# Modulation columns of a two-block transformer: raw fp32 weight blocks as the stationary operand instead of split weight rows

## The chip, the cores and the metric

The kernel runs on one core of one Trainium2 chip. The metric is the device time of one execution in microseconds (us). The engines are PE (TensorE, whose weight loads are listed apart as PEld), DVE (VectorE), ACT (ScalarE), POOL (GpSimd) and SP (SyncE, which issues most transfers). The kernel before took 1550.29 us in the median of three runs (1546.9 to 1552.76).

## The reference

Two transformer blocks of two layers each run over 512 tokens (and 256 context tokens) with 1024 features, all in fp32. The first block is modulated. For each of its two layers a condition vector of the tokens and one of the context give 3072 values each:

```
sc, scc = silu(c), silu(c_ctx)
mod   = sc  @ mod_w[i] + mod_b[i]        # [1024] @ [1024, 3072]
mod_c = scc @ mod_w[i] + mod_b[i]
shift, scale, gate = split(mod, 3)
h = rmsnorm(x) * (1 + scale) + shift     # input of the layer's projections
x = x + gate * (mix @ w_out)             # end of the layer
```

Layer AB (i = 0) has two dense attentions and updates tokens and context. Layer CD (i = 1) has a window attention and a short convolution and updates the tokens alone. The second block (an even layer, an odd layer, each with a per-layer embedding) has no modulation, and nothing in it changes.

## The kernel before

**Numbers and layout.** Activations stand feature-major, X[feature, token], each as two parts hi and lo in the reduced fp32r format. A projection multiplies three times per 128 features (hi by hi, lo by hi, hi by lo; lines 238 to 240). Weights arrive as raw fp32 pieces [128, 4, 256] of 512 KB through `weights` (line 210): SP issues the load into one of three buffers `raw`, ACT casts 512 columns to `wh` (line 229), DVE subtracts to get `wl` (line 232), and the raw buffer is free again.

**Modulation.** `mod_w` of a layer is cut into 12 chunks of 256 columns: 0 to 3 shift, 4 to 7 scale, 8 to 11 gate. A chunk is 1 MB, two raw pieces. It is used with the four columns `sc4` (hi and lo of the two conditions) as the stationary operand and 256 weight columns as the moving one: 16 matmuls (hi and lo of 8 feature blocks) into a PSUM row block [4, 256]. DVE copies it to `rows` (line 325 or 340), the bias is row 5, and two small fp32 matmuls with the 5 by 2 selector `sel2` (line 348) sum the parts and turn them into per-feature columns `modT`.

- Layer 0, chunks 0 to 7, run first in `start` (line 641), with buffers of their own: four `mraw`, five `mhi`, five `mlo` (`mod_load`, `mod_first`, lines 303 to 326; matmuls on line 323). The same stage norms and transposes the tokens (line 388), and scales and shifts them feature block by feature block (`fill`, lines 664 to 666). The first projection, `ab_first` (288 columns, 144 matmuls), can use a feature block as soon as it is filled.
- The other 16 chunks are fillers that use the general weight path (`mod_rows`, matmuls on lines 338 and 339): layer 1, chunks 0 to 7, and layer 0, gate chunks 8 to 11, lie between the projections of layer AB; layer 1, gate chunks 8 to 11, lie between items of layer CD's attention (`rest`, paced over 21 units).
- Gate rows take a trip through DRAM: `gate_rows` stores [5, 256] (line 357), `gate_sum` reads [5, 512], sums with `sel2` (line 364, 512 columns moving) and stores [2, 512] (line 366), and `gate_bc` reads one row broadcast to 128 partitions (line 370). `w_out` multiplies its result by the gate (line 906).

**Order.** The program is written in this order, and a scheduler with a model of its own lays out each engine's queue. On the chip each queue runs strictly in that order.

Of the kernel before, what the change touches and what calls it, by code (L numbers as in the profile page):

```python
# [29 lines left out]
class Kern:  # L30
# [55 lines left out]
    def psum(self, **banks):  # L86
        """the four banks beside the two pairs"""
        self.banks = banks
        self.pstack.close()
        self.ps = self.pstack.enter_context(self.pool("ps", space=PSUM))  # L90
# [9 lines left out]
    def setup(self, stack):  # L100
# [8 lines left out]
        self.grow_d, self.gsum_d = ([self.dram.tile([n, 1024], F32, name=f"g{n}row{l}_d") for l in range(2)] for n in (5, 2))  # L109
# [6 lines left out]
        self.sel2 = c.tile([5, 2], F32, name="sel2")  # L116
        nc.scalar.dma_start(out=self.sel2, in_=I["sel"])
        self.sc = c.tile([128, 8, 2], F32, name="sc")
        self.sc4 = c.tile([128, 8, 4], F32R, name="sc4")
        self.ng = c.tile([128, 2, 8], F32, name="ng")  # L120
        nc.scalar.dma_start(out=self.ng, in_=I["norm_g_2"])
        self.modT = [c.tile([128, 16, 2], F32, name=f"modT{l}") for l in range(2)]

    def gain_row(self, pool, name, tag, scale=None):
        """input row [1, n] on every partition"""
# [9 lines left out]
    def rstd(self, ms, n):  # L135
        """ms [128, n] mean squares -> (ms + eps)^-0.5"""
        self.nc.vector.tensor_scalar(out=ms, in0=ms, scalar1=EPS, scalar2=None, op0=ALU.add)  # L137
        self.nc.gpsimd.tensor_tensor(out=ms, in0=ms, in1=self.mhalf[:, 0:n], op=ALU.pow)  # L138
        return ms

    def split(self, src, hi, lo):
        """hi, lo (fp32r) of a fp32 AP (PSUM or SBUF)"""
# [16 lines left out]
    def silu2(self, ps, out):  # L159
        """out = 2*silu(ps)"""  # L160
# [4 lines left out]
    def head_norm(self, ps, H, d):  # L165
        """ps PSUM [128, T, H*d] -> normalised fp32 SBUF [128, T, H, d] (no gain)"""
# [18 lines left out]
    def rope(self, out, xn, C, S, r0, rot):  # L185
        """out = xn*C plus the rotary part on [r0, r0+rot), half-split pairs; C [128, T, d], S [128, T, rot]"""
# [12 lines left out]
    def gain_heads(self, out, xn, g):  # L199
        """out = xn*g over [128, T, H, d]"""  # L200
# [9 lines left out]
    def weights(self, ap):  # L210
        """ap DRAM [128, nk, n] -> [(k0, hi, lo)] pieces in fp32r"""
# [48 lines left out]
    def proj_feat(self, out, X, W, c0, t0, n):  # L260
        """feature-major block: out PSUM [128, n] = W[:, c0:c0+128]^T @ X[:, t0:t0+n]"""
# [20 lines left out]
    def feat(self, X, W, t=512):  # L282
        """feature blocks of a chunk over t tokens: yields (b, PSUM [128, n], t0, n)"""
# [9 lines left out]
    def load_silu_c(self):  # L293
# [7 lines left out]
        self.split(self.sc, self.sc4[:, :, 0:2], self.sc4[:, :, 2:4])  # L301

    def mod_load(self, layer, ch, pool):
        """the loads of a mod chunk, ahead of mod_first"""
        rows = self.tl(pool, [5, 256], "rows", 4)
        self.nc.scalar.dma_start(out=rows[4:5, :], in_=self.I["mod_b"][layer:layer + 1, 256 * ch:256 * ch + 256])
        raws = []
        for k in (0, 4):
            raws.append(self.tl(pool, [128, 4, 256], "mraw", 4))
            self.nc.sync.dma_start(out=raws[-1], in_=self.I["mod_w"][layer, ch][:, k:k + 4, :])  # L310
        return rows, raws

    def mod_first(self, ld, pool):
        """rows [5, 256] (x, ctx hi parts, lo parts, bias) of a loaded mod chunk"""
        nc = self.nc
        rows, raws = ld
        p = self.B()
        for kk in range(8):
            if kk % 2 == 0:
                hi, lo = (self.tl(pool, [128, 2, 256], x, 5, F32R) for x in ("mhi", "mlo"))  # L320
                self.split(raws[kk // 4][:, kk % 4:kk % 4 + 2, :], hi, lo)
            for j, w in enumerate((hi, lo)):
                nc.tensor.matmul(out=p[0:4, 0:256], lhsT=self.sc4[:, kk, :], rhs=w[:, kk % 2, :], start=kk + j == 0,
                                 stop=kk == 7 and j == 1)
        nc.vector.tensor_copy(out=rows[0:4, :], in_=p[0:4, 0:256])
        return rows, self.sel2

    def mod_rows(self, layer, ch):
        """rows [5, 256] (x, ctx hi parts, lo parts, bias) of mod chunk ch"""
        nc = self.nc  # L330
        W = self.weights(self.I["mod_w"][layer, ch])
        rows = self.T4([5, 256])
        nc.scalar.dma_start(out=rows[4:5, :], in_=self.I["mod_b"][layer:layer + 1, 256 * ch:256 * ch + 256])
        p = self.B()
        for k0, hi, lo in W:
            for k in range(hi.shape[1]):
                kk = k0 + k
                nc.tensor.matmul(out=p[0:4, 0:256], lhsT=self.sc4[:, kk, :], rhs=hi[:, k, :], start=kk == 0, stop=False)
                nc.tensor.matmul(out=p[0:4, 0:256], lhsT=self.sc4[:, kk, :], rhs=lo[:, k, :], start=False, stop=kk == 7)
        nc.vector.tensor_copy(out=rows[0:4, :], in_=p[0:4, 0:256])  # L340
        return rows, self.sel2

    def mod_cols(self, layer, ch, rs):
        """per-feature columns modT[layer][:, 2*ch + b, (x, ctx)]; the scales with one added"""
        rows, sel = rs
        p = self.B()
        for b in range(2):
            self.nc.tensor.matmul(out=p[:, 2 * b:2 * b + 2], lhsT=rows[:, 128 * b:128 * b + 128], rhs=sel)
        self.nc.vector.tensor_scalar(out=self.modT[layer][:, 2 * ch:2 * ch + 2, :].rearrange("p b e -> p (b e)"),
                                     in0=p[:, 0:4], scalar1=1.0, scalar2=1.0 if ch >= 4 else 0.0,  # L350
                                     op0=ALU.mult, op1=ALU.add)

    def gate_rows(self, layer, chs):
        """rows [5, 256] of the gate's chunks, spilled"""
        for h in chs:
            rows, _ = self.mod_rows(layer, 8 + h)
            self.nc.sync.dma_start(out=self.grow_d[layer][:, 256 * h:256 * h + 256], in_=rows)

    def gate_sum(self, layer, bank="F"):
        """rows [2, 1024] (x, ctx) of the gate from its spilled parts, spilled"""  # L360
        for h in (0, 512):
            rows, r, p = self.T4([5, 512]), self.T4([2, 512]), self.B(bank)
            self.nc.sync.dma_start(out=rows, in_=self.grow_d[layer][:, h:h + 512])
            self.nc.tensor.matmul(out=p[0:2, :], lhsT=self.sel2, rhs=rows)
            self.nc.scalar.copy(out=r, in_=p[0:2, :])
            self.nc.sync.dma_start(out=self.gsum_d[layer][:, h:h + 512], in_=r)

    def gate_bc(self, layer, out, which=0):
        """out[which] [128, 1024]: the gate (of x or ctx) broadcast over the partitions"""
        self.nc.sync.dma_start(out=out[which], in_=self.gsum_d[layer][which:which + 1, :].to_broadcast([128, 1024]))  # L370

# [10 lines left out]
    def transposes(self, xn, g):  # L382
        """PSUM [128, 2, 256]: feature blocks 2g, 2g+1 of two token tiles"""
# [8 lines left out]
    def feat_pair(self, xs, X, t0, scale=None, shift=None, norm=True):  # L392
        """xs: two [128, 1024] token tiles -> X[:, :, t0:t0+256] = (rms(x)*scale + shift)^T, split;
        scale(k), shift(k): per-feature columns"""
# [25 lines left out]
    def tr_pieces(self, src, T, d, fn, kind="R"):  # L420
        """transposes of token-major tiles src(t) [128, d] in PSUM pieces of up to 4 tiles: fn(piece, t0, n)"""
# [1340 lines left out]
def layout(inp):  # L1762
# [5 lines left out]
    d = {}  # L1768
# [73 lines left out]
```

## Time and profile before

| | |
|---|---|
| runs, median (lowest to highest) | 1550.29 us (1546.9 to 1552.76) |
| span of the profiled execution | 1546.3 us |
| its own time beside the span | not listed apart; the runs' median is 4.0 us above the span |
| PE busy, PEld busy | 1486.4 us (96%), 1373.0 us (89%) |
| DVE, ACT, POOL busy | 1036.5 us (67%), 846.5 us (55%), 546.9 us (35%) |
| chain that ended last | PE 79%, DVE 8%, DMA 5%, ACT 3% |
| moved by DMA | 168.20 MB, mean 109 GB/s |

Busy is the union of an engine's instructions. Matmuls overlap, so the time that one costs is the distance from its start to the start of the next, not its own length. A weight load (PEld) overlaps the matmul before it. PEclk is the clock granted to TensorE as a share of 2.4 GHz; it has two levels, 1.2 and 2.4 GHz. The first 19 us have no record of it, and the views print 1.00 there.

### The profile page before, as it was taken

The page shows a single profiled execution, that of the slowest core. Times are in us where ns is not written, and L with a number is a line of the kernel's source. Part 1 is how long each engine was busy: PE and PEld are TensorE (multiplying, and loading weights), DVE is VectorE, ACT ScalarE, POOL GpSimd, SP SyncE. Part 2 cuts the span into 40 slices and gives each one's busy share as a digit, 9 for nine tenths or more (in the row PEclk, how much of TensorE's full clock was granted, in tenths as well). Part 3 has the DMA queues.
Part 4 walks back from the last instruction along what each step waited for, and adds up shares of the span by engine and source line. Part 5 has one row for each costly group of instructions (what it writes and reads, how often), then busy time and mean ns, then how long its engine had stood idle before and what let it go on. Part 6 is the DMA issues. An engine that isn't in the chain of part 4 may idle for free.

```text
span 1546.3 us, 28606 instructions
## 1 busy us (share of the span) xinstructions
PE 1486.4 (96%) x10760; PEld 1373.0 (89%) x10760; DVE 1036.5 (67%) x2121; ACT 846.5 (55%) x1759; POOL 546.9 (35%) x652
## 2 busy tenths in 40 slices
PE   6899999989999999999999999999999999999998
PEld 3799788877998999888889889998899999998998
DVE  6777887889886477777755458986544465565444
ACT  6545555689996154565643446557433544455322
POOL 1533533567674033232421434444201334443000
PEclk8999999999999999999999999999999999999999
DMA  8344564121221332322234222124334321223423
GB/s 304 121 128 120 183 203 162 45 103 33 63 70 31 146 121 71 101 96 86 93 115 145 80 96 82 66 86 137 116 103 143 119 94 57 82 69 132 148 90 110
DMA packets 60685, 168.20 MB, mean 109 GB/s; under 512 B 9890, under 2 KB 18530, under 8 KB 60546
## 3 DMA queue, kind: packets, MB, share of 16 engines
q1 hardware_dynamic: 54768, 163.52, 31.8%
q10 hardware_dynamic: 5778, 2.84, 0.7%
q8 instruction: 85, 1.39, 0.4%
q14 instruction: 54, 0.44, 0.1%
HBM read 144.06 MB, written 22.28 MB: 108 GB/s over the span
## 4 chain that ended last, share of the span: by engine, by line
PE 79%; DVE 8%; DMA 5%; ACT 3%; issue 2%; POOL 2%; SPq 0%; ACTq 0%; DVEq 0%; POOLq 0%
PE A L240 17%; PE A L238 17%; PE A L239 17%; PE B L524 3%; PE F L238 3%; PE F L239 3%; PE F L240 3%; PE F L595 2%; PE B L238 2%; PE B L239 2%; PE B L240 2%; DVE wl L232 1%; PE B L996 1%; PE B L388 1%; PE B L1168 1%
## 5 line engine op out<-in xcount | busy, mean ns | idle before, releaser
L229 ACT CAST wh<-raw 128x512 fp32r<-128x512 f32 (+1 forms) x388 | 232.4, 616 | 237.8 <-PE A L240 166.9
L232 DVE TENSOR_TENSOR wl<-raw,wh 128x512 fp32r<-128x512 f32 (+1 forms) x320 | 233.4, 744 | 93.9 <-ACT wh L229 90.7
L481 POOL TENSOR_SCALAR P<-P,s 128x768 f32<-128x768 f32 (+3 forms) x192 | 152.8, 801 | 176.4 <-DVE s L1264 33.4
L144 DVE TENSOR_TENSOR PTl<-B,PTh 128x512 fp32r<-128x512 f32 (+2 forms) x208 | 127.9, 633 | 47.7 <-ACT PTh L143 35.0
L232 POOL TENSOR_TENSOR wl<-raw,wh 128x512 fp32r<-128x512 f32 x68 | 90.9, 1338 | 158.3 <-ACT wh L229 132.0
L138 POOL TENSOR_TENSOR s8f<-s8f,mhalf 128x4 f32<-128x4 f32 (+2 forms) x53 | 61.5, 1161 | 227.3 <-DVE s8f L137 119.7
L238 PE MATMUL A<-wh,mh 128*128 128x256 f32 x480 | 136.5, 285 | 2.9 <-ACT mh L143 2.9
L143 ACT CAST PTh<-B 128x512 fp32r<-128x512 f32 (+2 forms) x208 | 108.2, 545 | 53.8 <-PE B L524 27.1
L239 PE MATMUL A<-wl,mh 128*128 128x256 f32 x480 | 136.0, 284 | 0.0
L240 PE MATMUL A<-wh,g 128*128 128x256 f32 x408 | 115.7, 285 | 1.2 <-DVE g L144 1.2
L240 PE MATMUL A<-wh,h2l 128*128 128x256 f32 x384 | 108.7, 286 | 2.5 <-DVE h2l L408 2.5
L238 PE MATMUL A<-wh,h4h 128*128 128x256 f32 x384 | 109.5, 286 | 1.0 <-ACT h4h L407 0.8
L240 PE MATMUL A<-wh,h4l 128*128 128x256 f32 x384 | 108.7, 285 | 0.5 <-DVE h4l L408 0.5
L238 PE MATMUL A<-wh,h2h 128*128 128x256 f32 x384 | 108.9, 284 | 0.3 <-ACT h2h L407 0.3
L239 PE MATMUL A<-wl,h4h 128*128 128x256 f32 x384 | 108.7, 284 | 0.0
L239 PE MATMUL A<-wl,h2h 128*128 128x256 f32 x384 | 108.6, 283 | 0.0
L238 PEld LDWEIGHTS A<-wh,mh 128*128 128x128 f32 x480 | 91.9, 192 | 4.3 <-ACT mh L143 3.3
L239 PEld LDWEIGHTS A<-wl,mh 128*128 128x128 f32 x480 | 92.0, 192 | 0.1
L524 PE MATMUL B<-ident,P 128*128 128x128 f32 x592 | 86.2, 274 | 4.5 <-DVE PTl L144 2.4
L240 PEld LDWEIGHTS A<-wh,g 128*128 128x128 f32 x408 | 78.0, 192 | 1.7 <-DVE g L144 1.7
L490 ACT ACTIVATE P<-A,s 128x768 f32<-128x768 f32 (+1 forms) x96 | 73.2, 766 | 7.4 <-DVE s L488 4.7
L524 PEld LDWEIGHTS B<-ident,P 128*128 128x128 f32 x592 | 67.5, 141 | 9.2 <-POOL P L481 2.5
(515 smaller groups left out, 4914.8 us busy)
## 6 DMA issues: line engine op xcount, KB each, us to landing
raw<-mod_w SPq DMA_DIRECT2D x32, 512.0 KB
raw<-even_w SPq DMA_DIRECT2D x32, 512.0 KB
raw<-odd_w SPq DMA_DIRECT2D x32, 512.0 KB
raw<-cd_w SPq DMA_DIRECT2D x26, 512.0 KB
mraw<-mod_w SPq DMA_DIRECT2D x16, 512.0 KB
raw<-w_ple_gate SPq DMA_DIRECT2D x16, 512.0 KB
raw<-ab_wg SPq DMA_DIRECT2D x8, 512.0 KB
raw<-ab_wo SPq DMA_DIRECT2D x8, 512.0 KB
```

The costliest lines, as they stand in the source:

```text
L138: self.nc.gpsimd.tensor_tensor(out=ms, in0=ms, in1=self.mhalf[:, 0:n], op=ALU.pow)
L143: self.nc.scalar.copy(out=hi, in_=src)
L144: self.nc.vector.tensor_tensor(out=lo, in0=src, in1=f32(hi), op=ALU.subtract)
L229: nc.scalar.copy(out=hi, in_=r)
L232: eng.tensor_tensor(out=lo, in0=r, in1=f32(hi), op=ALU.subtract)
L238: mm(out=out, lhsT=xh, rhs=wh, start=start, stop=False)
L239: mm(out=out, lhsT=xh, rhs=wl, start=False, stop=False)
L240: mm(out=out, lhsT=xl, rhs=wh, start=False, stop=stop)
L481: self.nc.gpsimd.tensor_scalar(out=P, in0=P, scalar1=s, scalar2=0.0, op0=ALU.mult, op1=ALU.add)
L490: nc.scalar.activation(out=P[:, u, :], in_=S[:, u, :], func=AF.Exp, bias=m[:, u:u + 1], scale=1.0, accum_out=s[:, u:u + 1])
L524: nc.tensor.transpose(out=pt[:, j, u, :], in_=b, identity=self.ident)
L595: nc.tensor.matmul(out=O, lhsT=vst(e, j), rhs=pts[j // 2][w][:, j % 2], start=w + j == 0, stop=w == 1 and j == nk - 1)
```

## The change

The modulation no longer makes parts of its weights. A raw fp32 block of 128 features by 128 columns is now the stationary operand, and the two fp32 condition columns `sc` stream: 8 fp32 matmuls for each of the chunk's two column blocks, 16 in a chunk, straight into columns [128, 2]. Gone are the ACT casts and DVE subtractions of all 24 chunks, the rows, `sel2` and the DRAM trip. The bias is a table `mb` with one added to the scales beforehand, and one DVE addition writes `modT`, which now holds the gate's columns too. Chunks 0 to 7 of layer 0 have ten `mraw` buffers instead of four. The other 16 chunks take the three shared `raw` buffers, which PE reads directly. `gate_bc` spreads gate columns by four transposes for each half of the 1024 columns. (All comments were removed as well, so line numbers differ: 238 to 240 become 237 to 239, 388 becomes 353, 426 becomes 391.)

```diff
 # setup
-        self.grow_d, self.gsum_d = (...)
-        self.sel2 = c.tile([5, 2], F32, name="sel2")
-        self.sc4 = c.tile([128, 8, 4], F32R, name="sc4")
+        self.mb = c.tile([128, 2, 24], F32, name="mb")
+        nc.scalar.dma_start(out=self.mb, in_=I["mod_bt"])
+        nc.vector.tensor_scalar(out=self.mb[:, :, 8:16], in0=self.mb[:, :, 8:16], scalar1=1.0, scalar2=None, op0=ALU.add)
-        self.modT = [c.tile([128, 16, 2], F32, name=f"modT{l}") for l in range(2)]
+        self.modT = [c.tile([128, 24, 2], F32, name=f"modT{l}") for l in range(2)]
...
+    def mod_load(self, layer, ch, pool=None):
+        raws = []
         for k in (0, 4):
-            raws.append(self.tl(pool, [128, 4, 256], "mraw", 4))
+            raws.append(self.tl(self.rawp, [128, 4, 256], "raw") if pool is None else self.tl(pool, [128, 4, 256], "mraw", 10))
             self.nc.sync.dma_start(out=raws[-1], in_=self.I["mod_w"][layer, ch][:, k:k + 4, :])
...
-    def mod_first(self, ld, pool):
-    def mod_rows(self, layer, ch):
+    def mod_cols(self, layer, ch, raws):
         p = self.B()
         for b in range(2):
-            self.nc.tensor.matmul(out=p[:, 2 * b:2 * b + 2], lhsT=rows[:, 128 * b:128 * b + 128], rhs=sel)
+            for k in range(8):
+                self.nc.tensor.matmul(out=p[:, 2 * b:2 * b + 2], lhsT=raws[k // 4][:, k % 4, 128 * b:128 * b + 128],
+                                      rhs=self.sc[:, k, :], start=k == 0, stop=k == 7)
+        self.nc.vector.tensor_tensor(out=self.modT[layer][:, 2 * ch:2 * ch + 2, :],
+                                     in0=p[:, 0:4].rearrange("p (b e) -> p b e", b=2),
+                                     in1=self.mb[:, layer, 2 * ch:2 * ch + 2].unsqueeze(2).to_broadcast([128, 2, 2]), op=ALU.add)
-    def gate_rows(self, layer, chs):
-    def gate_sum(self, layer, bank="F"):
     def gate_bc(self, layer, out, which=0):
-        self.nc.sync.dma_start(out=out[which], in_=self.gsum_d[layer][which:which + 1, :].to_broadcast([128, 1024]))
+        for h in range(2):
+            t = self.T4([128, 512])
+            self.nc.vector.tensor_copy(out=t.rearrange("p (b f) -> p b f", b=4),
+                                       in_=self.modT[layer][:, 16 + 4 * h:20 + 4 * h, which].unsqueeze(2).to_broadcast([128, 4, 128]))
+            p = self.B("T")
+            for b in range(4):
+                c = slice(128 * b, 128 * b + 128)
+                self.nc.tensor.transpose(out=p[:, c], in_=t[:, c], identity=self.ident)
+            self.nc.scalar.copy(out=out[which][:, 512 * h:512 * h + 512], in_=p)
...
 # start
-            self.mod_cols(0, order[j], self.mod_first(lds[j], mp))
+            self.mod_cols(0, order[j], lds[j])
 # run: the calls between the projections of layer AB
-            self.gate_rows(0, range(4))
-            self.gate_sum(0)
+            self.mods(0, 8, 9, 10, 11)
 # run: layer CD
-                        self.gate_rows(1, (h,))
+                        self.mods(1, 8 + h)
-                self.gate_sum(1)
-            self.pace(items, ru, 21)
+            self.pace(items, ru, 20)
```

Where the queues change is seen at three places. On PE at the end of the first stage, `mhi` and `mlo` are the parts of a chunk, `hTh` is the filled input, and A is the first projection's PSUM. Before, the projections began between the matmuls of the third of the eight chunks:

```order
L323 MATMUL B_372<-mlo_382,sc_82 4x256
L323 MATMUL B_372<-mhi_389,sc_82 4x256
L238 MATMUL A_718<-wh_682,hTh_122 128x288
L323 MATMUL B_372<-mlo_390,sc_82 4x256
L323 MATMUL B_372<-mhi_389,sc_82 4x256
L323 MATMUL B_372<-mlo_390,sc_82 4x256
L323 MATMUL B_372<-mhi_397,sc_82 4x256
```

In the changed program the last of the eight chunks (B_444) ends, and then the first projection starts:

```order
L314 MATMUL B_444<-sc,mraw_414 128x2 x3
L314 MATMUL B_444<-sc,mraw_412 128x2 x4
L314 MATMUL B_444<-sc,mraw_414 128x2 x4
L237 MATMUL A_536<-wh_500,hTh_118 128x288
L238 MATMUL A_536<-wl_501,hTh_118 128x288
L353 MATMUL F_274<-ident,t_40_152 128x128
```

All projections now stand behind all eight chunks, and 40 of the 48 transposes of tokens stand among the chunks.

On PE at the gate chunks of layer 0 (F is the one PSUM bank of the fillers, B_2847 a projection of the latent attention), before:

```order
L338 MATMUL F_2980<-wh_2974,sc_82 4x256
L339 MATMUL F_2980<-wl_2975,sc_82 4x256
L238 MATMUL B_2847<-whf_2789,lTh_949 128x256
L239 MATMUL B_2847<-wlf_2790,lTh_949 128x256
L240 MATMUL B_2847<-whf_2789,lTl_950 128x256
```

The changed program has the last two gate chunks nearly side by side, with only transposes beside them:

```order
L391 MATMUL B_2987<-ident,q_1545 128x128 x4
L314 MATMUL F_2566<-sc,raw_2562 128x2 x4
L314 MATMUL F_2566<-sc,raw_2564 128x2 x4
L314 MATMUL F_2566<-sc,raw_2562 128x2 x4
L314 MATMUL F_2566<-sc,raw_2564 128x2 x4
L391 MATMUL B_2996<-ident,q_1545 128x128 x2
L314 MATMUL F_2588<-sc,raw_2584 128x2 x4
L314 MATMUL F_2588<-sc,raw_2586 128x2 x4
```

Each chunk now reads its two raw buffers twice, so both stay taken until its second half.

On SP's queue at the same place, before, stores of gate rows (`g5row_d`) stood between the loads:

```order
L357 DMA g5row_d<-t_592_2896 5x256
L222 DMA raw_3009<-mod_w 128x1024
L357 DMA g5row_d<-t_604_2937 5x256
L222 DMA raw_3054<-ab_wg 128x1024
L222 DMA raw_3064<-ab_wg 128x1024
L363 DMA t_630_3040<-g5row_d 5x512
```

Now five loads stand in a row, each waiting for one of three buffers that PE itself has to give back:

```order
L816 DMA qkv_d_96<-mk_2427 128x1152
L306 DMA raw_2564<-mod_w 128x1024
L306 DMA raw_2584<-mod_w 128x1024
L306 DMA raw_2586<-mod_w 128x1024
L221 DMA raw_2606<-ab_wg 128x1024
L221 DMA raw_2616<-ab_wg 128x1024
```

The row stores and sums are gone, and the load of the next gate projection's weights waits behind the chunks.

## Rows read from the trace of the kernel before

**Rows 1.** The page, part 1: busy us, share of the span, instructions of each engine.
```profile
PE 1486.4 (96%) x10760; PEld 1373.0 (89%) x10760; DVE 1036.5 (67%) x2121; ACT 846.5 (55%) x1759; POOL 546.9 (35%) x652
```
**Rows 2.** Busy time of each engine in stretches, with PEclk; columns in the first row.
```profile
core 0: us, PE busy (x) PEld busy (x) DVE busy (x) ACT busy (x) POOL busy (x), PEclk, DMA share, GB/s
20.00:80.00 60.00, 51.30 (x338) 42.40 (x339) 46.58 (x87) 37.90 (x74) 25.61 (x23) 0.86 0.56 188
80.00:240.00 160.00, 155.33 (x1109) 138.78 (x1109) 127.69 (x308) 85.70 (x171) 60.74 (x62) 1.00 0.51 163
600.00:790.00 190.00, 188.78 (x1105) 160.87 (x1105) 139.32 (x304) 111.22 (x244) 61.66 (x83) 1.00 0.26 86
```
**Rows 3.** PE's waits, 0 to 80: line waited for, total us, times, longest.
```profile
PE B L323 <- ACT mhi L143: 7.5, 2, 7.2
PE B L348 <- DVE rows L325: 3.6, 5, 2.1
PE B L323 <- DVE mlo L144: 3.1, 3, 2.1
```
**Rows 4.** PE's waits, 80 to 240 (first of five), then 600 to 790 (both).
```profile
PE A L240 <- DVE wl L232: 1.5, 1, 1.5
...
PE F L238 <- ACT cc L1017: 0.8, 1, 0.8
PE F L238 <- DVE t2f L340: 0.3, 1, 0.3
```
**Rows 5.** Timeline near the start: start us, length, engine, line, operation.
```profile
6.55 0.62 ACT L143 CAST mhi<-mraw 128x512 fp32r<-128x512 f32 x1 [2.31 <-DMA mraw<-mod_w]
8.34 0.41 PE L323 MATMUL B<-mlo,sc 128*4 128x256 f32 x1
8.55 0.41 PE L323 MATMUL B<-mhi,sc 128*4 128x256 f32 x1
11.81 0.92 PEld L348 LDWEIGHTS B<-sel,rows 5*128 5x128 f32 x4 [1.00 <-DVE rows L325]
```
**Rows 6.** Timeline at 103 to 105 us and at 235.7 us.
```profile
103.27 0.52 PEld L348 LDWEIGHTS F<-sel,t 5*128 5x128 f32 x4
104.03 0.28 PE L240 MATMUL A<-wh,hTl 128*128 128x256 f32 x1
104.15 0.28 PE L238 MATMUL A<-wh,hTh 128*128 128x256 f32 x1
...
235.72 1.01 PE L364 MATMUL F<-t,sel 5*2 5x512 f32 x2
236.66 0.73 PE L240 MATMUL A<-hTh,wl 128*128 128x512 f32 x2
```
**Rows 7.** Groups by form, PE and PEld: count, busy us, mean ns.
```profile
L348 PE MATMUL B<-sel,rows 5*128 5x2 f32 x32 | 5.5, 273 | 3.6 <-DVE rows L325 3.6
L239 PEld LDWEIGHTS A<-qk,qk 96*128 96x128 f32 x80 | 15.2, 190 | 1.3
L348 PEld LDWEIGHTS F<-sel,t 5*128 5x128 f32 x32 | 4.1, 185 | 1.7 <-DVE wl L232 0.4 <-DVE s8f L844 0.4 <-DVE g L163 0.2
```
**Rows 8.** Timeline: PE in the first projection, one early row and its last.
```profile
70.51 0.29 PE L238 MATMUL A<-wh,hTh 128*128 128x288 f32 x1
...
73.58 0.29 PE L240 MATMUL B<-wh,hTl 128*128 128x288 f32 x1
```
**Rows 9.** Stretches around one fall of the clock, columns as in rows 2.
```profile
74.00:77.00 3.00, 1.38 (x10) 0.71 (x9) 1.80 (x3) 1.93 (x4) 1.93 (x3) 1.00 0.63 210
77.00:81.00 4.00, 4.00 (x23) 4.00 (x22) 3.01 (x10) 3.25 (x9) 1.67 (x4) 0.57 0.80 299
81.00:100.00 19.00, 17.79 (x151) 17.26 (x151) 16.41 (x48) 9.19 (x20) 8.58 (x12) 1.00 0.34 96
```
**Rows 10.** By tile: the gate's use and its broadcast; ns min/median/max, first to last us.
```profile
L906 DVE TENSOR_TENSOR t<-A,gate x20: 680/683/692, 507.8 to 843.8; 128x512 f32<-128x512 f32 x20
L370 SPq DMA_DIRECT2D gate<-g2row_d x3: 325/326/430, 498.7 to 795.8; - x3
```

More of the change, by code (lines that the diff above doesn't have):

```diff
@@ L108, in setup @@
         self.dram = ent(self.pool("dram", space=DRAM))
-        self.grow_d, self.gsum_d = ([self.dram.tile([n, 1024], F32, name=f"g{n}row{l}_d") for l in range(2)] for n in (5, 2))
         self.rot_d = [self.dram.tile([128, 4, 2, n], F32, name=f"rot{n}_d") for n in (16, 32)]
@@ L115, in setup @@
         nc.vector.memset(self.mhalf, -0.5)
-        self.sel2 = c.tile([5, 2], F32, name="sel2")
-        nc.scalar.dma_start(out=self.sel2, in_=I["sel"])
         self.sc = c.tile([128, 8, 2], F32, name="sc")
-        self.sc4 = c.tile([128, 8, 4], F32R, name="sc4")
+        self.mb = c.tile([128, 2, 24], F32, name="mb")
+        nc.scalar.dma_start(out=self.mb, in_=I["mod_bt"])
+        nc.vector.tensor_scalar(out=self.mb[:, :, 8:16], in0=self.mb[:, :, 8:16], scalar1=1.0, scalar2=None, op0=ALU.add)
         self.ng = c.tile([128, 2, 8], F32, name="ng")
         nc.scalar.dma_start(out=self.ng, in_=I["norm_g_2"])
-        self.modT = [c.tile([128, 16, 2], F32, name=f"modT{l}") for l in range(2)]
+        self.modT = [c.tile([128, 24, 2], F32, name=f"modT{l}") for l in range(2)]
     def gain_row(self, pool, name, tag, scale=None):
@@ L300, in load_silu_c @@
         nc.vector.tensor_tensor(out=self.sc, in0=th, in1=ct, op=ALU.mult)
[L301 to L306, printed above, removed]
+    def mod_load(self, layer, ch, pool=None):
         raws = []
         for k in (0, 4):
-            raws.append(self.tl(pool, [128, 4, 256], "mraw", 4))
+            raws.append(self.tl(self.rawp, [128, 4, 256], "raw") if pool is None else self.tl(pool, [128, 4, 256], "mraw", 10))
@@ L310, in mod_load @@
             self.nc.sync.dma_start(out=raws[-1], in_=self.I["mod_w"][layer, ch][:, k:k + 4, :])
-        return rows, raws
-    def mod_first(self, ld, pool):
[L315 to L326, printed above, removed]
@@ L328, in mod_rows @@
-    def mod_rows(self, layer, ch):
[L330 to L341, printed above, removed]
@@ L343, in mod_cols @@
-    def mod_cols(self, layer, ch, rs):
-        rows, sel = rs
+        return raws
+    def mod_cols(self, layer, ch, raws):
         p = self.B()
         for b in range(2):
-            self.nc.tensor.matmul(out=p[:, 2 * b:2 * b + 2], lhsT=rows[:, 128 * b:128 * b + 128], rhs=sel)
-        self.nc.vector.tensor_scalar(out=self.modT[layer][:, 2 * ch:2 * ch + 2, :].rearrange("p b e -> p (b e)"),
-                                     in0=p[:, 0:4], scalar1=1.0, scalar2=1.0 if ch >= 4 else 0.0,
-                                     op0=ALU.mult, op1=ALU.add)
@@ L353, in gate_rows @@
-    def gate_rows(self, layer, chs):
-        for h in chs:
-            rows, _ = self.mod_rows(layer, 8 + h)
-            self.nc.sync.dma_start(out=self.grow_d[layer][:, 256 * h:256 * h + 256], in_=rows)
-    def gate_sum(self, layer, bank="F"):
[L361 to L366, printed above, removed]
@@ new lines, in mods @@
+    def mods(self, layer, *chs):
+        for ch in chs:
+            self.mod_cols(layer, ch, self.mod_load(layer, ch))
+    def gate_bc(self, layer, out, which=0):
+        for h in range(2):
[7 more added lines that the diff above has]
+            self.nc.scalar.copy(out=out[which][:, 512 * h:512 * h + 512], in_=p)
@@ L740, in ab_q @@
         return q
-    def mods(self, *chs):
-        for ch in chs:
-            self.mod_cols(1, ch, self.mod_rows(1, ch))
     def ab_lat(self, X, L, latg, between):
@@ L1479, in proj @@
                 self.banks["F"] = ("F", 1)
-            self.ab_lat(X, L, latg, lambda: self.mods(0, 1))
-            self.mods(2, 3)
+            self.ab_lat(X, L, latg, lambda: self.mods(1, 0, 1))
+            self.mods(1, 2, 3)
             proj(0)
@@ L1485, in run @@
             proj(1)
-            self.mods(4, 5)
+            self.mods(1, 4, 5)
             self.ab_gates(X, 2, keep(4))
             proj(2)
-            self.mods(6, 7)
+            self.mods(1, 6, 7)
             self.ab_gates(X, 3, keep(6))
             proj(3)
-            self.gate_rows(0, range(4))
-            self.gate_sum(0)
+            self.mods(0, 8, 9, 10, 11)
             self.ab_gates(X, 0, spill(0))
@@ L1639, in rest @@
                         yield
-                self.gate_sum(1)
-                yield
                 for b, p, t0, n in self.feat(Xx, self.weights(I["cd_w"][9])):
@@ L1770, in layout @@
     d["ct"] = A(np.stack([g["c"][0], g["c_ctx"]], -1).reshape(8, 128, 2).transpose(1, 0, 2))
-    d["mod_w"], d["mod_b"] = np.stack([chunks(w) for w in g["mod_w"]]), A(g["mod_b"])
+    d["mod_w"] = np.stack([chunks(w) for w in g["mod_w"]])
+    d["mod_bt"] = A(g["mod_b"].reshape(2, 24, 128).transpose(2, 0, 1))
     ab = g["ab_w_in"][0]
@@ L1809, in layout @@
     d["rope_ab"] = A(rope.reshape(4, 128, -1).transpose(1, 0, 2))
-    d["sel"] = np.array([[1, 0], [0, 1], [1, 0], [0, 1], [1, 1]], f)
     neg = f(-1e30)
```

## The prediction

> **What bounds the kernel now.** I read the page's busy times first. The reader is to see PE at 96% and every other engine far below [rows 1]. Then the stretches: from 80 to 240 us and from 600 to 790 us, where 16 of the 24 chunks are worked, PE is busy for 155.33 of 160 and 188.78 of 190 us at the full clock [rows 2]. Before 80 us it is not the only bound: PE has 51.30 of 60 us and a mean clock of 0.86. The waits say who feeds PE. Up to 80 us the splits and row copies of the modulation make it wait 7.5, 3.6 and 3.1 us, 14.2 us in all [rows 3]; from 80 to 240 us there are five waits with 4.5 us together, the longest 1.5, and from 600 to 790 us two with 1.1 us [rows 4]. So behind 80 us what the change frees on ACT and DVE is worth little, and what it adds on PE counts almost one for one.
>
> **PE's price of a chunk.** Before, a chunk is 16 matmuls of 256 columns. At the full clock one follows another after 0.12 us (104.03 to 104.15) [rows 6]: 1.9 us. The new matmul has not run here with 128 rows, but its form has: the selector matmul is plain fp32, 128 stationary columns, two moving columns. It shows 32 loads and 32 matmuls on each bank where the program has 16 (eight chunks, two each) [rows 7]: one fp32 matmul becomes two loads and two matmuls. Four loads take 0.52 us, the last being 0.185 long, so the spacing is (0.52 - 0.185) / 3 = 0.112 us [rows 6, 7]. That the selector has 5 rows and the weights 128 should not matter: a load of 96 rows and 128 columns has 190 ns, one of 5 rows and 128 columns 185 [rows 7]. So a chunk becomes 32 pairs, 32 x 0.112 = 3.6 us at the full clock. At the lower clock four loads take 0.92 us, and matmuls of 256 columns lie 0.21 us apart instead of 0.12 [rows 5, 6]: I take 0.22 for a pair and 7.0 us for a chunk.
>
> **The 16 chunks behind 80 us, at the full clock.** Added: 16 x 3.6 = 57.3 us, and 24 gate transposes, priced as one 128-column load each, 2.7 us. Removed: 256 matmuls x 0.12 = 30.7 us; the selectors of eight chunks, 32 x 0.112 = 3.6 us; the gate sums, eight instructions at (236.66 - 235.72) / 2 = 0.47, 3.8 us [rows 6]. Sum: +22 us. The new matmuls stand as solid blocks of 16, so no other engine's work covers them. Bounds: +15 if a matmul follows a load some 10% sooner than the selector's, +30 if the turn to other work adds 0.5 us a chunk.
>
> By the Trainium skill's page Perfetto Trace Analysis, section "Identifying the Most-Contended Engine", it is the busy share of weight loads that tells PE's room, and not that of matmuls. That share is 89% here [rows 1]; if the 11% left took up these loads, the +22 would be 0. The added loads come in blocks, and the waits in these stretches sum to 5.6 us, so I don't go by it.
>
> **The clock behind 80 us.** From 74 to 77 us PE had 1.38 us of work in 3, and from 77 to 81 the mean granted clock is 0.57; in 81 to 100, with PE working all along, it is 1.00 again [rows 9]. That fall cost 4.00 x 0.43 = 1.7 us. A new chunk keeps the loader busy but streams two columns per load. No row shows loads alone. I expect the clock to treat such a block as idleness. Eight blocks stand alone or first in their group: 1.7 us each. The other eight follow another within some 30 instructions, as the last gate chunks do, and meet the lower clock: half of their pairs at double price (1.8) and 1.7 more, 3.5 us. Together 42, taken as +40 us. Bounds: 0, and 16 x (3.6 + 1.7) = 85 if every block runs wholly at 1.2 GHz.
>
> **The first stage.** PE can begin at 6.6 us, when the first cast began for its landed load [rows 5]. Now it holds eight chunks and 40 transposes ahead of the first projection. Nothing in them streams, so I expect 1.2 GHz throughout: 8 x 7.0 + 40 x 0.22 = 64.8 us, to 71.4 us. Then 144 matmuls of 288 columns, 0.133 us each ((73.58 - 70.51) / 23) [rows 8], 19.2 us, eight transposes 0.9, and 2 us until the clock is up: 93.5 us, where the trace has 73.9. That is +20 us, although the 14.2 us of waits are gone: before, most of the projection ran between the chunks. Bounds: -12 (2.4 GHz nearly from the start: 6.6 + 28.7 + 4.5 + 2 + 20.1 = 62) and +25.
>
> **Smaller terms.** Relief of ACT and DVE: -4, bounds 0 and the 5.6 us of waits. The raw buffers: a chunk reads its first piece until three quarters of it and the second to the end, and SP's queue now has five loads behind one another, each waiting for PE; the next gate projection's weights stand behind them, and `qkv_d` stores too. A load from issue to use took some 4 us at the start (the first cast began at 6.55) [rows 5], a chunk takes 3.6 to 7, so most of it hides: +4, bounds 0 and +20. The DRAM trip: 0. The broadcasts were issued from 498.7 us, the gate is first used at 507.8 [rows 10]; now DVE's copy and ACT's copy for each half lie beside projections. The longer use of PSUM bank F: 0, since one use replaces two.
>
> **Sum.** 22 + 40 + 20 - 4 + 4 = +82 us on a span of 1546.3, so 1628; the runs' median lies 4 us above that span, and the forecast is 1632 us.
>
> **Rivals.**
> (1) The clock stays up, because loads count as work. For it: PE never waits in these blocks. Against it: nothing here shows it either way but the fall after thin work. The start gains 12, the relief 4, the rest costs 22, and the buffers, with nothing to hide them, 7: +13, 1563 us. The Trainium skill's page TensorE: Matmul & The Clock Gate, Part 1, says the gate sets the clock by how busy PE has been; read so that loads are busy, it speaks for this rival. No run here shows a stretch of loads alone.
> (2) The clock is low in the first stage only, and the blocks later are too short to bring it down: 20 + 22 - 4 + 5 = +43, 1593 us. For it: each block is 3.6 us with dense work on both sides. Against it: gate chunks side by side.
> (3) Faster. A matmul with 128 rows needs one load and not two, so a chunk is 16 x 0.112 = 1.8 us. Behind 80 us: 28.7 + 2.7 - 38.1 = -7; the first stage at 1.2 GHz ends 28 us sooner, -8; relief -4, buffers +4: -15, 1535 us; with the clock up throughout 1525. It decides where a pair costs under 0.07 us. Against it: two loads for one selector matmul.
>
> **How the numbers follow.** Forecast 60%, its own range 1600 to 1660; rival 1 18%, with a spread of 15 us around 1563; rival 2 12%; rival 3 7%; 3% for worse than the forecast's range. The range to 80% reaches down into rival 1: 1560 to 1665. A measurement of this kernel can tell about 0.5%, 7.8 us. Faster by more: rival 3 and nothing else, 0.07. Within: the lower edge of rival 1, 0.06. Slower: 0.87.
>
> **What would show it.** The new matmul line should have 768 matmuls and 768 loads, 0.11 us apart at the full clock and 0.22 in the first stage. PEclk should stand near half up to some 75 us, and below 1 in the slices around the chunks. The last 288-column matmul should come near 93 us. ACT's and DVE's share should fall while PE's waits hardly change. The forecast is wrong if PEclk is full while the chunks run, if a matmul shows one load, or if PE waits for raw loads more than 20 us.

## The result and the profile after

The changed kernel takes 1619.34 us (median of 4 runs, 1613.01 to 1622.0) beside 1548.6 us before (4 runs, 1546.44 to 1552.76): a ratio of 1.044, 95% interval 1.0418 to 1.0462, so 70.7 us slower. The forecast was 1632 us. The profiled execution has a span of 1611.2 us, 64.9 more than before's 1546.3; parts below are in terms of these two spans. The profiled execution is the fastest of the four, with a mean granted clock of 0.972; the other three have 0.965 to 0.970 and are 5.6 to 9.0 us longer, so a typical run pays more for the clock than the parts below show.

The page of the changed kernel, busy us with share of the span and count, and the row of the clock in 40 slices of 40.3 us:

```profile
PE 1560.9 (97%) x11096; PEld 1472.1 (91%) x11096; DVE 971.1 (60%) x2015; ACT 796.8 (49%) x1664; POOL 529.2 (33%) x652
...
PEclk9998897999999999998899999999999999999999
```

Beside [rows 1], PE has 74.5 us more, DVE 65 us and ACT 50 us less. The digit of the clock is below 9 in slices 4, 5, 7, 19 and 20 (121 to 201, 242 to 282 and 725 to 806 us), which is where most of the 16 later chunks stand.

The changed kernel by source line, for the new matmul's line: engine, operation, tiles, count, then duration in ns (min/median/max), first and last start, and below what stood idle ahead of it and until what (us, times; this list counts a wait of the loads and one of the matmuls behind them as two):

```profile
L314 PEld LDWEIGHTS F<-sc,raw x512: 186/192/338, 109.9 to 802.2; 128*128 128x128 f32 x171
L314 PE MATMUL F<-sc,raw x512: 165/251/373, 110.0 to 802.3; 128*128 128x2 f32 x171
L314 PEld LDWEIGHTS B<-sc,mraw x256: 288/333/370, 7.7 to 69.4; 128*128 128x128 f32 x128
L314 PE MATMUL B<-sc,mraw x256: 213/352/353, 7.7 to 69.5; 128*128 128x2 f32 x128
...
  DMA mraw<-mod_w: 7.7, 1
  issue: 7.7, 1
  DMA raw<-mod_w: 4.4, 2
  DVE modT L316: 2.1, 2
```

There are 512 + 256 = 768 loads and 768 matmuls for 384 in the program, so each fp32 matmul became two of both, as read from the selector [rows 7]. The eight chunks of the first stage (B) have loads of 333 ns, the later ones (F) 192.

PE on the changed kernel's timeline (start, us, line, tiles, count), in the first stage, at the end of the first projection, and in the first two later chunks:

```profile
42.50 5.12 PE L314 MATMUL B<-sc,mraw 128*128 128x2 f32 x24
47.48 0.88 PE L353 MATMUL F<-ident,t 128*128 128x128 f32 x3
...
91.50 0.30 PE L239 MATMUL B<-wh,hTl 128*128 128x288 f32 x1
...
110.81 3.19 PE L314 MATMUL F<-sc,raw 128*128 128x2 f32 x28
114.35 1.21 PE L726 MATMUL B<-ident,t 128*128 128x128 f32 x4 [0.36 <-DVE t L721]
115.35 2.99 PE L314 MATMUL F<-sc,raw 128*128 128x2 f32 x14
```

At 110.8 us 28 matmuls take 3.19 us, (3.19 - 0.25) / 27 = 0.109 us each: the full clock. At 42.5 us 24 take 5.12, (5.12 - 0.35) / 23 = 0.207: the lower clock. At 115.4 us, one chunk later, 14 take 2.99, (2.99 - 0.35) / 13 = 0.203. These means are a little low, because the first step behind other work is short (0.03 us at the full clock, 0.07 at the lower). Step by step, nearly all matmuls of the new line follow one another after 0.111 or 0.112 us at the full clock and after 0.213 at the lower one. So the block at 110.8 us ran at 2.4 GHz and the next one at 1.2. The last matmul of 288 columns starts at 91.5 us; before it was at 73.6 [rows 8].

Busy time of each engine in the changed kernel in the stretches of [rows 2], and one more around the two chunks above:

```profile
core 0: us, PE busy (x) PEld busy (x) DVE busy (x) ACT busy (x) POOL busy (x), PEclk, DMA share, GB/s
20.00:80.00 60.00, 60.00 (x303) 59.98 (x304) 17.78 (x39) 17.45 (x32) 11.26 (x12) 1.00 0.37 146
80.00:240.00 160.00, 158.04 (x1118) 153.33 (x1117) 95.34 (x246) 58.14 (x120) 61.66 (x71) 0.90 0.39 132
600.00:790.00 190.00, 182.10 (x1154) 164.12 (x1153) 126.68 (x269) 91.20 (x195) 51.92 (x69) 0.96 0.25 82
109.00:125.00 16.00, 15.64 (x97) 15.39 (x96) 4.74 (x11) 4.34 (x8) 0.69 (x1) 0.68 0.40 132
```

From 80 to 240 us the clock is 0.90 and from 600 to 790 0.96, where both were 1.00 [rows 2]. The 1.00 of the first stretch is not a reading: this execution has no record of the clock until 73.6 us, and views print 1.00 where there is none. The step of 0.213 us is what tells the clock there: it is the step that the same pairs have where the record shows 1.2 GHz. The loader is busy for 59.98 of 60 us in it.

**Where the 64.9 us are.** I cut both traces at matmuls that exist in both, and counted each matmul in between at its full-clock step (work; 0.1186 us for 256 columns, 0.233 for 512, 0.112 for a new pair). Where the clock record or the spacing shows 1.2 GHz I added what its step is longer there (clock; 0.213 instead of 0.1186, 0.427 instead of 0.233, 0.213 instead of 0.112), and took the rest as waiting. In us, after minus before:

| stretch, ending at | length | work | clock | waiting |
|---|---|---|---|---|
| last 288-column matmul | +17.9 | +9.9 | +22.8 | -14.8 |
| the rest of the AB projections (280 to 328 us) | +30.1 | +16.0 | +22.3 | -8.2 |
| dense attention and `w_out` of AB, gate transposes | +3.0 | +1.5 | +1.5 | 0.0 |
| layer CD, to its last projection (793 to 862 us) | +18.2 | +5.8 | +10.1 | +2.3 |
| everything behind it | -4.4 | +0.9 | -2.0 | -3.2 |

### The profile page after: what moved, and what is told of

The parts are those of the page before. It is cut to its first block, busy times and chain, and to the rows that moved or that the text cites. A ratio compares the mean times of both kernels' runs of the same rounds, so it can differ in the third digit from the quotient of the medians.

```text
span 1611.2 us, 28851 instructions
## 1 busy us (share of the span) xinstructions
PE 1560.9 (97%) x11096; PEld 1472.1 (91%) x11096; DVE 971.1 (60%) x2015; ACT 796.8 (49%) x1664; POOL 529.2 (33%) x652
## 4 chain that ended last, share of the span: by engine, by line
PE 76%; DVE 7%; DMA 4%; ACT 4%; issue 2%; POOL 2%; SPq 0%; ACTq 0%; DVEq 0%; POOLq 0%
PE A L237 16%; PE A L239 16%; PE A L238 16%; PE B L489 3%; PE F L314 3%; PE F L237 3%; PE F L238 3%; PE F L239 3%; PE F L560 2%; PE B L237 1%; PE B L238 1%; PE B L239 1%; DMA raw<-cd_w 1%; DVE wl L231 1%; PE B L956 1%
## 5 line engine op out<-in xcount | busy, mean ns | idle before, releaser
L228 ACT CAST wh<-raw 128x512 fp32r<-128x512 f32 (+1 forms) x324 | 195.0, 614 | 246.7 <-PE A L239 152.2
L231 DVE TENSOR_TENSOR wl<-raw,wh 128x512 fp32r<-128x512 f32 (+1 forms) x256 | 187.0, 745 | 125.8 <-ACT wh L228 116.4
L446 POOL TENSOR_SCALAR P<-P,s 128x768 f32<-128x768 f32 (+3 forms) x192 | 147.3, 773 | 268.2 <-DVE s L938 72.9
```

The source lines that it names most:

```text
L228: nc.scalar.copy(out=hi, in_=r)
L231: eng.tensor_tensor(out=lo, in0=r, in1=f32(hi), op=ALU.subtract)
L446: self.nc.gpsimd.tensor_scalar(out=P, in0=P, scalar1=s, scalar2=0.0, op0=ALU.mult, op1=ALU.add)
```

## The experiments

The theory: a chunk costs PE two loads for each matmul, and blocks of such loads that stream two columns bring the clock to 1.2 GHz, in them and on either side. The rivals: PE waits for raw buffers and the DMA queue; the first stage is late because projections stand behind all eight chunks, whatever the clock; and, once the first runs were in, that something moves the whole program which is neither.

### One suspected cost taken away: more columns under the same loads

After, and each new matmul streams the two columns 64 times over, 128 columns in all; the loads and the buffers are as in after. The scheduler laid PE's queue out anew for it: some 600 of the 11,096 matmuls stand at another place, and 2 of the 144 matmuls of the first projection now stand ahead of the last chunk's end.

```diff
-                self.nc.tensor.matmul(out=p[:, 2 * b:2 * b + 2], lhsT=raws[k // 4][:, k % 4, 128 * b:128 * b + 128],
-                                      rhs=self.sc[:, k, :], start=k == 0, stop=k == 7)
+                self.nc.tensor.matmul(out=p[:, 256 * b:256 * b + 128].rearrange("p (r e) -> p r e", e=2), lhsT=...,
+                                      rhs=self.sc[:, k, :].unsqueeze(1).to_broadcast([128, 64, 2]), start=k == 0, stop=k == 7)
```

> The changed kernel, but each modulation matmul streams 128 columns instead of two: the two condition columns read 64 times over (a stride of zero), of which only the first two results are used. Loads, order of the code and buffers stay. Theory (the clock falls because these blocks stream almost nothing): PEclk is near 1 in the first stage and in all chunks, a pair costs 0.11 to 0.12 us everywhere, the last 288-column matmul comes at 61 to 66 us instead of 91.5, the half-clock time of about 39 us behind it goes, together -60 to -68 us: 1551 to 1560 us. Rival A (double loads and their place in the order are the whole cost, the clock follows from something else): within 8 us of 1619. Rival B (the loss behind 90 us is PE waiting for raw buffers that it holds itself): the first stage gains 28, the rest stays: about 1590.

Measured: 1565.33 us (1559.6 to 1566.82), ratio to before 1.0083 (1.0056 to 1.011), 54 us less than after; mean clock 0.993 where after has 0.972 (without a record for its first 73.6 us, which count as full there). This kernel's stretches, its new line in the first stage, a chunk, and its last 288-column matmul:

```profile
20.00:80.00 60.00, 58.37 (x484) 57.59 (x483) 35.98 (x84) 25.61 (x51) 26.67 (x34) 1.00 0.51 183
80.00:240.00 160.00, 151.45 (x1129) 143.40 (x1127) 93.06 (x231) 59.23 (x122) 52.97 (x54) 0.99 0.47 152
```
```profile
L314 PEld LDWEIGHTS B<-sc,mraw x256: 188/191/333, 7.8 to 47.4; 128*128 128x128 f32 x128
L314 PE MATMUL B<-sc,mraw x256: 272/273/551, 7.8 to 47.5; 128*128 128x128 f32 x128
```
```profile
66.44 0.29 PE L239 MATMUL B<-wh,hTl 128*128 128x288 f32 x1
...
86.05 2.62 PE L314 MATMUL F<-sc,raw 128*128 128x128 f32 x22
```

The reader sees the same 256 loads end at 47.4 us and not at 69.4, with 191 ns each and not 333, and 0.99 in the second stretch. A pair costs (2.62 - 0.27) / 21 = 0.112 us, as it did at the full clock with two columns: the spacing shows no price for 126 more columns under each load. So 54 of the 71 us are the clock, and the clock came back with more columns streamed, with not one load less. The other order of PE's queue is not kept apart by this run; the two kernels with only the first stage changed, further below, do that. It missed the range of its expectation by 5 us upward, and the last 288-column matmul by 0.4 us. PE's waits for raw loads rose to 5.0 us in four waits (there was one of 2.2). That faster blocks ask for the next buffer sooner would explain it; no run tests it.

### One part alone: the later chunks

After, with chunks 0 to 7 of layer 0 made as before (splits, rows, selector).

```diff
-            self.mod_cols(0, order[j], lds[j])
+            self.mod_cols0(0, order[j], self.mod_first(lds[j], mp))   # both as before the change
```

> The first stage as before (splits, rows, selector); only the 16 later chunks and the gates in the new form. Theory: 22 us of PE work at the full clock and 30 to 40 for falls of the clock, less the 4 us of relief: +45 to +55, 1594 to 1604 us, with PEclk below 1 only around the chunks. Rival (waits for raw buffers): PE's waits on lines of the chunks and of weight casts between 74 and 300 us sum to over 15 us and PEclk falls there because of them.

Measured: 1592.07 us (1589.23 to 1593.49), ratio 1.026 (1.0238 to 1.0282). Its stretches and its longest waits of PE from 80 to 330 us (line waited for, total us, times, longest):

```profile
80.00:240.00 160.00, 159.46 (x1108) 154.38 (x1108) 92.91 (x241) 58.10 (x117) 59.79 (x65) 0.88 0.42 139
600.00:790.00 190.00, 184.25 (x1099) 165.24 (x1098) 119.52 (x263) 89.24 (x194) 50.70 (x71) 0.93 0.25 80
```
```profile
PE B L430 <- DVE kB L456: 2.1, 1, 2.1
PE B L528 <- POOL P L485: 1.6, 1, 1.6
PE B L599 <- DVE PTl L146: 1.1, 1, 1.1
...
PE F L318 <- DMA raw<-mod_w: 0.3, 1, 0.3
```

The last 288-column matmul comes at 74.5 us, about as before (73.6), and the stretches behind it show the low clock of after. That is +40 us against before for the 16 chunks, 2 us below the expected range. PE waited 0.8 us on lines of the chunks, 0.3 of it for raw loads, where the rival wanted over 15, so the raw buffers are neither what costs the time nor what brings the clock down. (Tiles lie elsewhere here than in before, and that alone moves the time, as the section on SBUF shows: the mean step of 256 columns is 117.4 ns here and 118.6 in before, which over some 6,600 steps is 8 us in favour of this kernel.)

### The other part alone: the first stage

Before, with chunks 0 to 7 of layer 0 in the new form (ten `mraw` buffers, the bias table, no rows), the later ones as they were.

```diff
-            self.mod_cols(0, order[j], self.mod_first(lds[j], mp))
+            self.mod_raw(0, order[j], lds[j])          # the new mod_cols
```

> Only chunks 0 to 7 of layer 0 in the new form with two streamed columns; the other 16 chunks and the gates as before. Theory: only the first stage's loss, the last 288-column matmul at 91 us instead of 73.6, +18: 1567 us. Rival (the loss comes from the scheduler's other order as a whole): no fixed share, the time off by more than 8 us from 1567.

Measured: 1550.48 us (1545.19 to 1554.34, 10 runs), ratio 0.9997 (0.9978 to 1.0015): no change, where 1567 was expected. This is the run that the theory could not explain. Its first stage and last 288-column matmul:

```profile
20.00:80.00 60.00, 60.00 (x310) 59.98 (x311) 18.12 (x37) 16.65 (x31) 11.96 (x12) 1.00 0.37 144
```
```profile
89.93 0.29 PE L243 MATMUL B<-wh,hTl 128*128 128x288 f32 x1
```

The first stage did lose 16.3 us (89.9 for 73.6), as in after. The rest of the program gave it back. It has the same 10,408 matmuls as before, in the same order but for some 180, nearly all of them between 74 and 106 us.

### The same with more columns

The kernel just told of, streaming 128 columns per load as above.

```diff
-                nc.tensor.matmul(..., rhs=self.sc[:, k, :], ...)
+                nc.tensor.matmul(..., rhs=self.sc[:, k, :].unsqueeze(1).to_broadcast([128, 64, 2]), ...)
```

> As the kernel with only the first stage changed, but streaming 128 columns there. Theory: the first stage runs at the full clock, the last 288-column matmul at 61 to 66 us instead of 73.6 in the kernel before, nothing later changes: -8 to -12, 1537 to 1541 us, faster than both kernels. Rival A (clock not the cause): as the kernel with two columns, 1567. Rival C (the stage is then bound by the transfers of 8 MB of weights and 3 MB of tokens): last 288-column matmul between 66 and 74 us, 1541 to 1549.

Measured: 1525.93 us (1524.95 to 1527.39), ratio 0.9839 (0.9816 to 0.9862), the fastest of all versions. Its first stage, the new line in it and its last 288-column matmul:

```profile
20.00:80.00 60.00, 59.70 (x488) 59.70 (x489) 37.72 (x85) 27.41 (x53) 27.39 (x33) 0.97 0.54 198
```
```profile
L317 PEld LDWEIGHTS B<-sc,mraw x256: 186/192/337, 6.4 to 46.7; 128*128 128x128 f32 x128
```
```profile
66.21 0.30 PE L243 MATMUL B<-wh,hTl 128*128 128x288 f32 x1
```

The last 288-column matmul came at 66.2 us where it had been at 89.9. In both kernels all 144 matmuls of the projection stand behind all eight chunks, and some 80 matmuls in all stand elsewhere, so it is the clock that cost the time in the first stage and not the order. 66.2 is also where rival C's range begins, but PE was busy for 59.70 of 60 us there, so the transfers were not what held it. The whole came again some 12 us sooner than its expectation. Both runs that were too fast share a table of 192 B per partition at the front of SBUF that before doesn't have.

### Where things lie in SBUF

Before, plus that table, unused: all tiles behind it lie 192 B higher, and nothing else of the computation changes.

```diff
+        self.mb = c.tile([128, 2, 24], F32, name="mb")
+        nc.scalar.dma_start(out=self.mb, in_=I["mod_bt"])
+        nc.vector.tensor_scalar(out=self.mb[:, :, 8:16], in0=self.mb[:, :, 8:16], scalar1=1.0, ...)
```

> The kernel before, computing all as before; only the bias table of the change (192 bytes on every partition, loaded, one added to the scales, then used by nothing) is added, so that everything behind it in SBUF lies as far on as in the kernel with only its first stage changed. That kernel lost 16 us in the first stage and was as fast as before at its end. Theory P (where things lie in SBUF sets the spacing of the matmuls of the second block, 0.116 us there against 0.119 to 0.120 before): 8 to 12 us faster than before, 1538 to 1543 us, the segment from the first matmul on the second block's input to the end shorter by about 8 us. Rival Q (the gain behind the first stage comes from other engines being ahead, or from other executions): same as before within 4 us.

Measured: 1536.3 us (1533.36 to 1538.65), ratio 0.9912 (0.9897 to 0.9928). An unused table makes before 13.4 us faster, 2 us beyond the expected range, with PE's 10,760 matmuls in the same order.

After, plus an unused tile of 8 B, by which later tiles lie 32 B higher:

```diff
+        self.sel2 = c.tile([128, 2], F32, name="sel2")
+        nc.vector.memset(self.sel2, 1.0)
```

> The changed kernel with 8 bytes per partition more (one unused small tile), so that all behind it lies 32 bytes on; PE's queue is unchanged. Theory P: the spacing in the second block changes with it, and the time by some 4 to 10 us either way from 1619. Rival Q: 1619 within 4 us. The theory on the clock expects no change in the first stage (last 288-column matmul at 91 to 92 us) and at the later chunks in both cases.

Measured: 1607.86 us (1605.66 to 1608.86), ratio to before 1.0369 (1.0351 to 1.0388), 11.5 us less than after, just beyond the expected 4 to 10. Its first stage did not move (last 288-column matmul at 91.1 us).

Three more on before tell the place from the added instructions. An unused tile of 192 B filled by one memset; the memset of another tile given twice, with no place moved; and the unused tile with 32 B.

```diff
+        self.pad = c.tile([128, 48], F32, name="pad")     # 192 B; in the third kernel [128, 8], 32 B
+        nc.vector.memset(self.pad, 1.0)
```
```diff
         nc.vector.memset(self.mhalf, -0.5)
+        nc.vector.memset(self.mhalf, -0.5)
```

> The kernel before, with one unused 192 B tile per partition allocated where e6 put its table, filled once by a memset; no added load. Theory P (addresses in SBUF decide): the same shift of 192 B as e6, so the same gain, 1534 to 1540 us, and 256-column matmuls of the h4 group mostly 0.113 us apart. Rival Q (something else that e6 added, its load or its extra instructions, moves the program): no change, 1546 to 1553 us, 0.120 us apart.

> The kernel before, with the first memset of the constant tile given twice: one instruction more on DVE, no address moved in SBUF. Theory P (addresses in SBUF decide): no change, 1546 to 1553 us, matmuls of the h4 group 0.120 us apart. Rival Q (one instruction more moves the program, and that decides): 1534 to 1540 us, 0.113 us apart.

> The kernel before, with an unused tile of 32 B per partition in place of the 192 B of e8. Theory P (addresses in SBUF decide) says only that some shifts gain and some don't: either 1534 to 1540 us as with 192 B (any move off the old place gains) or 1544 to 1553 us (only certain places gain). Rival Q (the added instruction decides): the same time as e8 and e9.

Measured: 1539.45 us (ratio 0.9908, 0.9877 to 0.994) with 192 B, 1552.3 us (0.9999, 0.9982 to 1.0016) with the extra instruction, 1544.69 us (0.9962, 0.9945 to 0.9979) with 32 B. The place decides, and the instruction does nothing; 32 B fell between, just inside the range I had given to "no gain", so a shift is not all or nothing. PE's timeline in the same projection of the second block, with the extra instruction and then with 192 B:

```profile
1306.69 0.28 PE L239 MATMUL A<-wh,h4h 128*128 128x256 f32 x1
1306.81 0.28 PE L240 MATMUL A<-wl,h4h 128*128 128x256 f32 x1
1306.93 0.28 PE L241 MATMUL A<-wh,h4l 128*128 128x256 f32 x1
1307.05 0.28 PE L239 MATMUL A<-wh,h4h 128*128 128x256 f32 x1
1307.17 0.28 PE L240 MATMUL A<-wl,h4h 128*128 128x256 f32 x1
```
```profile
1305.26 0.28 PE L240 MATMUL A<-wh,h4h 128*128 128x256 f32 x1
1305.38 0.28 PE L241 MATMUL A<-wl,h4h 128*128 128x256 f32 x1
1305.49 0.28 PE L242 MATMUL A<-wh,h4l 128*128 128x256 f32 x1
1305.60 0.28 PE L240 MATMUL A<-wh,h4h 128*128 128x256 f32 x1
1305.72 0.28 PE L241 MATMUL A<-wl,h4h 128*128 128x256 f32 x1
```

Four steps take 0.48 us in the one and 0.46 in the other: 0.120 and 0.115 us for the same matmul, with no wait in either; the expectation had 0.113 for the second. Over all neighbours of 256 columns in a trace at the full clock (steps under 0.15 us), some 6,500 to 6,900 in each kernel, the mean spacing is:

| kernel | mean spacing, ns | median of the runs, us |
|---|---|---|
| before / extra instruction | 118.6 / 118.6 | 1549.67 / 1552.3 |
| before, 32 B | 117.5 | 1544.69 |
| before, 192 B by the tile / by the table | 116.5 / 116.3 | 1539.45 / 1536.3 |
| before, first stage alone, two columns / 128 | 116.4 / 116.6 | 1550.48 / 1525.93 |
| after | 117.9 | 1619.34 |
| after, 32 B | 116.3 | 1607.86 |

Some 6,870 matmuls by 118.6 - 116.3 = 2.3 ns are 15.8 us, beside 13.4 measured; 32 B on before gives 1.1 ns, 7.5 us, beside 6.3 measured; 32 B on after gives 6,550 by 1.6 ns, 10.5 us, beside 11.5. So the spacing carries this effect in the medians. Single executions scatter around it: the profiled spans of after and of after with 32 B lie only 4.1 us apart (1611.2 and 1607.1), and the record of the second shows the lower clock for 109 us behind the first projection where the first has 92. Which of the moved tiles matters, and why, stays open.

Between kernels of nearly equal spacing (116.3 to 116.6 ns) the theory's sizes come out: the first stage alone costs 1550.48 - 1536.3 = +14.2 us with two columns (expected +18) and 1525.93 - 1536.3 = -10.4 with 128 (expected -8 to -12), and the whole change 1607.86 - 1536.3 = +71.6.

## Why the prediction was right, step by step

The time fell in the forecast's own range, 12.7 us below the 1632 that it named, and the mechanism was the one forecast. Three terms were off: the clock and the waits were smaller than forecast, and the place in SBUF was not in the sum.

**PE's price of a chunk** was right: two loads and two matmuls, 0.112 us a pair at the full clock as forecast, 0.213 at the lower beside 0.22. That 5 rows and 128 cost the same held.

**The 16 chunks at the full clock**, +22 with 24 gate transposes: the table's work behind the first stage is 16.0 + 1.5 + 5.8 + 0.9 = +24.2. The Trainium skill's page Perfetto Trace Analysis, section "Identifying the Most-Contended Engine", would have PE's room read from the busy share of loads, beside the share of the peak rate reached; that busy share rose from 89% to 91% only, and the 24.2 us were paid nonetheless. The kernel with 128 columns, where the clock hardly falls, shows the stretches of the AB projections and of layer CD 15.6 and 7.0 us longer than before. Here the share over the whole span told nothing of the room beside a solid block.

**The clock behind 80 us**, +40: 22.3 + 10.1 = +32.4 around the chunks in this execution, and more in the three longer ones. Most blocks did not fall themselves: 113 of their 512 pairs ran at the lower clock (forecast: half the pairs of eight blocks, 128), 88 of them in the chunk at 115.4 us and in the last two gate chunks of layer 0. The rest of the price was paid by other work behind the blocks. That it is the clock is shown by the kernels with 128 columns: 54 us less than after, and 24.6 us less where only the first stage is changed (1550.48 and 1525.93). The Trainium skill's page TensorE: Matmul & The Clock Gate, Part 1, says that the gate follows how busy PE has been. PEld was busy for 59.98 of 60 us in the first stage, at a step that only the lower clock gives, so here busy can't be read as loads in progress; with 128 columns under them the same loads ran at 2.4 GHz.

**The first stage**, +20: +17.9, the last 288-column matmul at 91.5 us beside 93.5 forecast. Lower clock throughout and the waits of 14.2 us gone, both as put. The 2 us that the forecast gave the clock to come back had no row behind them; after, 12 matmuls of the projection and 4 transposes ran at the lower clock until 73.6 us, which cost 1.7. It was the clock and not the order: with 128 columns, and all but two or all of the projection's matmuls still behind the eight chunks, the stage ends at 66.4 and 66.2 us.

**The raw buffers**, +4, and **the relief of ACT and DVE**, -4 (bounds 0 and -5.6), were 0 together. What the view names for PE's waits in the AB projections, before, after, and in the kernel with 128 columns (first lines of each):

```profile
PE A L240 <- DVE wl L232: 1.5, 1, 1.5
PE A L238 <- ACT pk L702: 1.4, 1, 1.4
PE B L238 <- ACT t2f L825: 1.3, 2, 1.1
```
```profile
PE F L314 <- DMA raw<-mod_w: 2.2, 1, 2.2
PE F L314 <- DVE modT L316: 0.8, 1, 0.8
```
```profile
PE F L314 <- DMA raw<-mod_w: 5.0, 4, 1.9
PE F L314 <- DVE modT L316: 1.4, 3, 0.9
```

Before, all 7.8 us of named waits are for ACT and DVE. After, 1.8 us of these are left, and 2.9 with 128 columns: the relief was 6.0 and 4.9 us, as put or somewhat more. The new lines' own waits came to 3.0 and 6.4 us: the raw buffers cost about what was put. What went wrong is the part that the view names no cause for. The rest between matmuls in this stretch is 13.9 us before, 5.7 after and 13.8 with 128 columns; less the named waits, 6.1, 0.9 and 4.5 us of it are left. So the waiting is 8.2 us less after, and the same as before with 128 columns. **The sum of the waits is the term that was mis-sized**: forecast 0, found -8.2 + 2.3 = -5.9. One reading is that a block at the lower clock lets the other engines get ahead, so that part of the clock's price is paid by gaps that it closes, and then the terms were not to be added as if they were independent. No run tests this by itself.

**What the prediction had not thought of** is the place in SBUF. Removing `sel2` and `sc4` and adding `mb` moved later tiles. In the stretch behind layer CD, where the change touches nothing but the last gate transposes, the mean spacing fell from 118.8 to 117.8 ns, which over some 4,160 steps is 3.9 us, and the lower clock cost 2.0 us less in this execution; 0.9 us of transposes came on top, and the stretch gained 4.4. That the removed and added tiles did it is taken over from the kernels that only move tiles; it was not tested on this pair.

Together: +82 forecast on the span, +64.9 found. The work behind the first stage took 2.2 us more than forecast (24.2 for 22), the clock there 8.1 less (31.9 for 40), the first stage 2.1 less (17.9 for 20), and the waits behind it, shorter steps among them, 9.1 less (-9.1 for 0). The place did not decide: the changed kernel with its tiles 32 B on, 1607.86 us, lies in the forecast's own range (1600 to 1660) too.

**The rivals.** Rival 1 had said 1563 us if the clock stays up, and the kernel with 128 columns, where it does, takes 1565.33: the rival's total was right and its condition false. In part the total is luck, since the start gained 7.1 us there (66.4 for 73.6) where the rival had 12. Rival 2 needed a full clock in the later chunks; those show 0.90 and 0.96. Rival 3 needed one load per matmul; there are two.

## What to carry to other kernels

Before weights are made stationary for a few moving columns, ask what such a block does to the clock: here it cost 54 of the 71 us. A load leaves room for streaming: here 126 repeated columns under each load cost nothing that the spacing shows (0.112 us with 2 and with 128) and kept 2.4 GHz, and with the first stage alone in that form the kernel beat the one before (1525.93 us, of which 10.4 us are that form's and the rest the place in SBUF). And when an edit moves a tile near the front of SBUF, compare with a version that has only that move: here it was worth up to 13 us, enough to hide a loss of 14.

## What the runs showed of the hardware that was not expected

- An unused tile of 192 B per partition ahead of the others brought the mean spacing of 256-column matmuls from 118.6 to 116.5 ns and took 0.9% off the time, with every matmul in the same order.
- The loader at work for 59.98 of 60 us with two columns streamed per load ran at 1.2 GHz (0.213 us a pair); with 128 columns per load at 2.4 GHz (0.112 us).
- The clock row of the profile printed 9 where the execution has no record at all: up to 73.6 us in the changed kernel. The spacing of equal matmuls tells the clock there.
